# Where the weight buffers and the token buffers start within a partition

## The chip, the core and the metric

The kernel runs on one core of a Trainium2 chip. The metric is the device time of one execution in microseconds (us), the median of three runs; smaller is better. The engines are TensorE (PE for its matmuls, PEld for its weight loads), VectorE (DVE), ScalarE (ACT), GpSimd (POOL) and SyncE (SP), which issues most transfers.

## The reference, cut to what matters

The program is a two-layer decoder trunk on 512 tokens of width 1024. Each layer is a half-step feed-forward block, a mixing block (attention heads with an output projection) and a second feed-forward block, each followed by a normalisation:

```python
def swiglu(x, w_gu, w_down):
    g, u = jnp.split(x @ w_gu, 2, axis=-1)
    return (jax.nn.silu(g) * u) @ w_down

for layer in range(DEPTH):                       # DEPTH = 2
    x = layer_norm(DN_ALPHA * x + 0.5 * swiglu(x, ffn_w_gu[layer, 0], ffn_w_down[layer, 0]), ...)
    ...                                          # layer 0: latent attention; layer 1: sparse attention
    x = layer_norm(DN_ALPHA * x + mix, ...)
    x = layer_norm(DN_ALPHA * x + 0.5 * swiglu(x, ffn_w_gu[layer, 1], ffn_w_down[layer, 1]), ...)
```

All data is float32. The hidden width of the feed-forward block is 2816, or 22 blocks of 128.

## The kernel before, in words

**Precision.** Every large product is made of float32 numbers split into a high and a low part (`split`, L198 and L199: ACT rounds the high part, DVE subtracts it), and three of the four partial products are summed in PSUM. So one product is three matmuls: high by high, high by low, low by high.

**Weights.** `load` brings one unit of weights, 128 partitions by 1024 numbers, into one of the four buffers of `wraw`; `prep` splits it into a pair `whi`, `wlo` out of `wring` (three pairs) or, inside a scope, out of `wx` (four more pairs). `ahead` keeps this a few units in front of TensorE.

**Feed-forward.** For most blocks of 128 hidden features `seven` makes the gate and up products in quarters, by a scheme of seven products instead of eight, from sums of the weights and sums of the tokens (`token_forms`, the tiles named `t`): `quarter` (L366, L367, L370) runs matmuls whose stationary operand is a 128x128 piece of `whi` or `wlo` and whose moving operand is 256 tokens of `xhi`, `xlo` or a form `t`. The other blocks go through `feature_major` (L353, L355, L358), with the same roles. The down product goes through `prod` (L401 to L406): there the stationary operand is a piece of the hidden activations (`hhi`, `hlo`) and the moving operand is 512 columns of `whi` or `wlo`. The output projection of the mixing block uses `prod` too, with the tiles `mix` as stationary operand. Where it is the last tile of 128 tokens that is projected, the same products are written with `mm3` (L345 to L347).

**Where the buffers lie.** A partition holds 448 times 512 bytes. Pools stack up from the bottom (left side) or from the top (right side), each tile as long as its row, and the addresses below are those of the program as built. From the bottom lie a 4096-byte ring of descriptors (`DMA_RING`), four one-number constants of 32 bytes each, then `cst` (400 numbers, 1600 bytes) and `cbf` (384 bf16 numbers, 768 bytes). `wraw` therefore starts at 4096 + 128 + 1600 + 768 = 6592, which is 448 above a multiple of 512 (64 below the next). Every later tile on the left up to the extra pairs `wx` is a multiple of 512 bytes long, so all of `wraw`, `whi` and `wlo` start 448 above a multiple of 512, and so do the tiles of the attention heads that are opened on the left (`ke`, `ko`, `qt`, `va`, `sv`, `skc`, `pp`). In `open_f` a tile of 64 bytes named `offset` lies at the bottom of `xp`, in front of the tokens: `x`, `xhi`, `xlo`, the norm's gains and the forms `t` come out at 448 + 64 = 512, that is at a multiple of 512. On the right, `hhi`, `hlo`, `mix`, `cT` and the memory's `mhi`, `mlo` start at multiples of 512 and `qf` at 448. Below, the offset of a tile is its start modulo 512, and a pair such as 0/448 names the moving operand's offset first and the stationary operand's second. Inside a tile the matmuls begin at whole multiples of 512 bytes from its start, other than for the weights `wc` and `wgq`.

**Order.** The program places instructions in the order in which it is written; each engine runs its own in that order. The first transfer of `cst` is issued from POOL, and the bf16 copies `cbf` (L1252, L1253 in the trace) are made from it by DVE at the start.

Of the kernel before, what the change touches and what calls it, by code (L numbers as in the profile page):

```python
# [9 lines left out]
F32 = mybir.dt.float32  # L10
# [7 lines left out]
P = 128  # L18
# [85 lines left out]
def tile_trunk(ctx: ExitStack, tc, a: dict, out):  # L104
    nc = tc.nc
    order = _unit_order()

    const = ctx.enter_context(tc.tile_pool(name="const", bufs=1))
# [96 lines left out]
    def zero(t):  # L205
        nc.vector.memset(t.bitcast(F32), 0.0)

    cst = const.tile([P, 400], F32, name="cst")
    nc.gpsimd.dma_start(cst[:, 0:400], a["cst"])
    ident = cst[:, 0:128]  # L210
    valid = cst[:, 384:385]
    cbf = const.tile([P, 384], BF16, name="cbf")
    identb = cbf[:, 0:128]
    maskb = cbf[:, 128:256]
    maskb2 = cbf[:, 128:384]
    mhalf = cst[:, 385:387]

    class F:
        pass
# [1090 lines left out]
def _slopes(n):  # L1310
    def pow2(k):
        s = 2.0 ** (-8.0 / k)
        return [s ** (i + 1) for i in range(k)]
    c = 2 ** math.floor(math.log2(n))
    return np.asarray(pow2(c) + pow2(2 * c)[0::2][:n - c], np.float32)


def _round12(v):

    m, e = np.frexp(np.asarray(v, np.float64))  # L1320
    return np.ldexp(np.round(m * 4096.0) / 4096.0, e)


def _constants():

    f = np.float32
    c = {}
    cst = np.zeros((P, 400), f)
    cst[:, 0:128] = np.eye(P)
    i = np.arange(P)  # L1330
    cst[:, 128:256] = np.where(i[None, :] <= i[:, None], 0.0, NEG)
    cst[:, 384] = (i >= 31)
    cst[:, 385:387] = -0.5
    c["cst"] = cst

    freq = (f(10000.0) ** (-np.arange(16, dtype=f) / f(16))).astype(f)
    ang = (np.arange(T, dtype=f)[:, None] * freq[None, :]).astype(f)
    co, si = np.cos(ang.astype(np.float64)), np.sin(ang.astype(np.float64))
    rope = np.zeros((P, 2, NT, 32), f)
    ct = np.concatenate([co, co], 1).reshape(NT, P, 32).transpose(1, 0, 2)  # L1340
    sn = np.concatenate([-si, si], 1).reshape(NT, P, 32).transpose(1, 0, 2)
    rope[:, 0], rope[:, 1] = ct, sn
    c["rope"] = rope
    sc = 96.0 ** -0.5
    cs = np.zeros((P, 2, T), f)
    cosr = np.concatenate([co, co], 1).T * sc
    sinr = np.concatenate([-si, si], 1).T * sc
    cs[0:64, 0] = sc
    cs[64:96, 0], cs[96:128, 0] = cosr, sinr
    cs[0:32, 1], cs[32:64, 1] = cosr, sinr  # L1350
    cs[64:128, 1] = sc
    c["cs"] = cs

    pos = np.zeros(NKEY)
    for j in range(NT):
        for r in range(2):
            o = 256 * j + 128 * r
            pos[o:o + 128] = 128 * j + np.arange(128)
    alk = np.zeros((P, NKEY), f)
    for base in (0, 64):  # L1360
        for r in range(4):
            alk[base + r] = pos - (128 * r + 64)
        alk[base + 4:base + 6] = 1.0
        alk[base + 6:base + 12] = alk[base:base + 6]
    c["alk"] = alk
    m = _slopes(HEADS).astype(np.float64)
    tq = np.arange(T)
    alq = np.zeros((HEADS, 64, T), f)
    for h in range(HEADS):
        mh = _round12(m[h])  # L1370
        for r in range(4):
            alq[h, r] = np.where(tq // 128 == r, mh, 0.0)
            alq[h, 6 + r] = np.where(tq // 128 == r, m[h] - mh, 0.0)
        v = -m[h] * (tq - (128 * (tq // 128) + 64.0))
        v1 = _round12(v)
        v2 = _round12(v - v1)
        alq[h, 4], alq[h, 10] = v1, v2
        alq[h, 5] = _round12(v - v1 - v2)
    n = np.arange(32, dtype=f)
    dist = tq.astype(f)[:, None] - (n[None, :] * f(16.0) + f(15.5))  # L1380
    ok = (16 * n[None, :] + 31 <= tq[:, None]) & (n[None, :] < 31)
    alc = np.where(ok[:, None, :], -_slopes(HEADS)[None, :, None] * dist[:, None, :], f(NEG)).astype(f)
    c["alc"] = alc.reshape(NT, P, 2, 3, 2, 32).transpose(3, 1, 0, 4, 2, 5).reshape(3, P, T)
    c["alq"] = alq
    return c


def _layout(inp):
# [47 lines left out]
    o["cpos"] = g["cmp_pos"].reshape(2, 16, P).transpose(2, 0, 1)  # L1436
    o["cmp_b1"] = g["cmp_b1"].reshape(1, 2, 256)
    o.update(_constants())
    return {k: np.ascontiguousarray(v) for k, v in o.items()}

# [15 lines left out]
```

## Time and profile before

| what | value |
|---|---|
| median of 3 runs | 1913.37 us (1911.97 to 1915.62) |
| the profiled execution's own time | 1914.72 us |
| its span, from the first instruction to the last | 1912.8 us |
| TensorE's mean granted clock, as a share of full speed | 0.996 |
| PE busy, share of the span | 98% |
| PEld busy, share of the span | 87% |
| DVE / ACT / POOL busy, share of the span | 77% / 45% / 9% |
| matmuls | 12560 |

The busy time of a matmul in the profile overlaps with that of its neighbours, because matmuls are pipelined: what counts for the time is the distance from the start of one matmul to the start of the next. That distance is called the spacing below. It is read from the start times of a listing in order of time, or from the number of matmuls in a window of the trace. Such a number includes the one or two that were under way when the window began.

### The profile page before, as it was taken

Reading aid. Unit: us, or ns where it says so; the run is one execution under the profiler, and the core shown is the slowest. Engines: PE = TensorE matmul, PEld = TensorE weight load, DVE = VectorE, ACT = ScalarE, POOL = GpSimd, SP = SyncE. Lnnn points to the kernel's source line nnn. Section 1 sums busy time; section 2 is a strip of 40 time slices with the busy share of each in tenths; the row PEclk is TensorE's granted clock in tenths of the full one; section 3 lists DMA queues with packets and bytes.
Section 4 is the critical chain, followed back from the end, with each engine's and each line's share of the span. In section 5 each row is a group of like instructions: output and inputs, shape, how many; then the busy total and the mean of one; then the engine's idle time right before and its main releaser. Section 6 shows DMA issues by size and latency. Waiting matters only on the chain.

```text
span 1912.8 us, 31481 instructions
## 1 busy us (share of the span) xinstructions
PE 1883.7 (98%) x12560; PEld 1666.8 (87%) x12560; DVE 1470.0 (77%) x2363; ACT 870.1 (45%) x1435; POOL 164.3 (9%) x185
## 2 busy tenths in 40 slices
PE   9999999999999999999999999999999999999998
PEld 8899899886679899899989998998856689999997
DVE  7798788757658779778787987977477377887886
ACT  5344344446545335334653433444466344434432
POOL 0000000025500000000100000001255200000000
PEclk9999999999999999999999999999999999999999
DMA  6333334530134234234333323334421224323322
GB/s 235 111 111 101 120 100 143 174 106 32 59 110 134 77 100 133 78 100 144 123 110 110 121 87 100 122 105 161 111 45 27 101 77 132 105 84 111 113 79 74
DMA packets 59715, 203.88 MB, mean 107 GB/s; under 512 B 6945, under 2 KB 7217, under 8 KB 59569
## 3 DMA queue, kind: packets, MB, share of 16 engines
q1 hardware_dynamic: 57136, 194.70, 31.3%
q0 software_dynamic: 2432, 7.17, 1.2%
q8 instruction: 99, 1.62, 0.3%
q14 instruction: 48, 0.39, 0.1%
HBM read 188.21 MB, written 7.34 MB: 102 GB/s over the span
## 4 chain that ended last, share of the span: by engine, by line
PE 92%; DVE 3%; ACT 2%; issue 2%; POOL 1%; DMA 1%; POOLq 0%; DVEq 0%; ACTq 0%
PE bank L366 13%; PE bank L370 13%; PE bank L367 13%; PE bank L402 5%; PE bank L403 5%; PE bank L405 5%; PE bank L404 5%; PE bank L401 5%; PE bank L406 5%; PE bank L358 3%; PE bank L355 3%; PE bank L353 3%; PE o L634 3%; PE tb L606 3%; PE s L1136 1%
## 5 line engine op out<-in xcount | busy, mean ns | idle before, releaser
L198 ACT CAST whi<-wraw 128x1024 fp32r<-128x1024 f32 (+3 forms) x479 | 463.2, 974 | 585.9 <-PE bank L406 263.1
L199 DVE TENSOR_TENSOR wlo<-wraw,whi 128x1024 fp32r<-128x1024 f32 (+3 forms) x479 | 536.9, 1125 | 135.0 <-ACT whi L198 127.0
L366 PE MATMUL bank<-t,whi 128*128 128x256 f32 x1232 | 303.8, 279 | 0.0
L367 PE MATMUL bank<-t,whi 128*128 128x256 f32 x1232 | 303.6, 279 | 0.0
L366 PEld LDWEIGHTS bank<-t,whi 128*128 128x128 f32 x1232 | 231.1, 188 | 0.0
L367 PEld LDWEIGHTS bank<-t,whi 128*128 128x128 f32 x1232 | 231.0, 188 | 0.0
L366 PE MATMUL bank<-xhi,whi 128*128 128x256 f32 x924 | 227.9, 280 | 0.0
L367 PE MATMUL bank<-xlo,whi 128*128 128x256 f32 x924 | 227.7, 279 | 0.0
L370 PE MATMUL bank<-t,wlo 128*128 128x256 f32 x1232 | 194.8, 279 | 0.0
L366 PEld LDWEIGHTS bank<-xhi,whi 128*128 128x128 f32 x924 | 173.3, 188 | 0.8
L367 PEld LDWEIGHTS bank<-xlo,whi 128*128 128x128 f32 x924 | 173.3, 188 | 0.8
L370 PEld LDWEIGHTS bank<-t,wlo 128*128 128x128 f32 x1232 | 166.7, 188 | 0.0
L309 DVE SCALAR_TENSOR_TENSOR x<-x,bank 128x512 f32<-128x512 f32 x176 | 112.6, 682 | 70.3 <-PE bank L405 66.2
L370 PE MATMUL bank<-xhi,wlo 128*128 128x256 f32 x924 | 146.1, 279 | 0.0
L404 PE MATMUL bank<-wlo,hhi 128*128 128x512 f32 x336 | 132.9, 395 | 0.0
L402 PE MATMUL bank<-whi,hhi 128*128 128x512 f32 x336 | 132.7, 395 | 0.0
L406 PE MATMUL bank<-whi,hlo 128*128 128x512 f32 x336 | 132.7, 395 | 0.0
L405 PE MATMUL bank<-whi,hlo 128*128 128x512 f32 x336 | 132.5, 394 | 0.0
L403 PE MATMUL bank<-wlo,hhi 128*128 128x512 f32 x336 | 132.4, 394 | 0.0
L401 PE MATMUL bank<-whi,hhi 128*128 128x512 f32 x336 | 132.3, 394 | 0.0
L353 PE MATMUL bank<-xhi,whi 128*128 128x256 f32 (+1 forms) x472 | 127.8, 302 | 2.0 <-ACT xhi L198 2.0
L355 PE MATMUL bank<-xlo,whi 128*128 128x256 f32 (+1 forms) x472 | 127.6, 302 | 0.6 <-DVE xlo L199 0.6
(331 smaller groups left out, 3520.2 us busy)
## 6 DMA issues: line engine op xcount, KB each, us to landing
wraw<-in_gu SPq DMA_DIRECT2D x175, 512.0 KB, 3.4
wraw<-in_dn SPq DMA_DIRECT2D x88, 512.0 KB, 3.9
wraw<-in_wo SPq DMA_DIRECT2D x16, 512.0 KB, 3.6
wraw<-in_wm SPq DMA_DIRECT2D x8, 512.0 KB, 4.1
x_dram<-x SPq DMA_DIRECT2D x8, 512.0 KB, 2.8
x<-x_dram SPq DMA_DIRECT2D x8, 512.0 KB, 4.3
wraw<-in_w SPq DMA_DIRECT2D x8, 512.0 KB, 4.5
wraw<-in_wq SPq DMA_DIRECT2D x6, 512.0 KB, 4.2
```

Of the source, the lines that this page charges most:

```text
L198: nc.scalar.copy(hi, src)
L199: eng.tensor_tensor(lo, src, hi.bitcast(F32), op=ALU.subtract)
L353: nc.tensor.matmul(ps[:, c0:c1], lhsT=hi[:, k * P:(k + 1) * P], rhs=F.xhi[:, k, c0:c1], start=k == 0, stop=False)
L366: nc.tensor.matmul(ps, lhsT=hi[:, ks], rhs=xh[:, k], start=k == 0, stop=False)
L367: nc.tensor.matmul(ps, lhsT=hi[:, ks], rhs=xl[:, k], start=False, stop=False)
L370: nc.tensor.matmul(ps, lhsT=lo[:, ks], rhs=xh[:, k], start=False, stop=k == 3)
L401: nc.tensor.matmul(p0, lhsT=ahi, rhs=hi[:, 0:512], start=first, stop=False)
L402: nc.tensor.matmul(p1, lhsT=ahi, rhs=hi[:, 512:1024], start=first, stop=False)
L403: nc.tensor.matmul(p0, lhsT=ahi, rhs=lo[:, 0:512], start=False, stop=False)
L404: nc.tensor.matmul(p1, lhsT=ahi, rhs=lo[:, 512:1024], start=False, stop=False)
L405: nc.tensor.matmul(p0, lhsT=alo, rhs=hi[:, 0:512], start=False, stop=last)
L406: nc.tensor.matmul(p1, lhsT=alo, rhs=hi[:, 512:1024], start=False, stop=last)
```

## The change

The constants' tile `cst` loses the 128 columns (256 to 383) that nothing reads, and 16 columns that held three numbers are kept behind the rest, so that it has 288 columns, or 1152 bytes, instead of 400, or 1600 bytes. The transfer that fills it is as much smaller: 147,456 bytes instead of 204,800. No instruction is added or removed, and none changes its order.

By that every tile on the left behind `cst` starts 448 bytes lower: `wraw` at 6144, a multiple of 512, and so `whi`, `wlo`, and the heads' tiles on the left; the tokens `x`, `xhi`, `xlo` and the forms `t` come out 64 above a multiple of 512. Nothing moves on the right.

```diff
-    cst = const.tile([P, 400], F32, name="cst")
-    nc.gpsimd.dma_start(cst[:, 0:400], a["cst"])
+    cst = const.tile([P, 288], F32, name="cst")
+    nc.gpsimd.dma_start(cst, a["cst"])
     ident = cst[:, 0:128]
-    valid = cst[:, 384:385]
+    valid = cst[:, 256:257]
...
-    mhalf = cst[:, 385:387]
+    mhalf = cst[:, 257:259]
...
-    cst = np.zeros((P, 400), f)
+    cst = np.zeros((P, 288), f)
...
-    cst[:, 384] = (i >= 31)
-    cst[:, 385:387] = -0.5
+    cst[:, 256] = (i >= 31)
+    cst[:, 257:259] = -0.5
```

The pairs of offsets, moving/stationary, before and after:

| matmuls | before | after |
|---|---|---|
| gate and up: L366, L367, L370, L353, L355, L358 | 0/448 | 64/0 |
| down and output projection: L401 to L406, and `mm3` with `hhi`, `mix` | 448/0 | 0/0 |
| memory keys; memory values | 0/448; 448/0 | 0/0; 0/0 |
| `wc` (the two halves of a unit) | 448/0 and 64/0 | 0/64 and 128/64 |
| block scores with `skc`, `qf` | 448/448 | 448/0 |

## Rows read from the trace of the kernel before

**Rows 1.** The page: span and busiest engine (busy us, share, instructions).

```profile
span 1912.8 us, 31481 instructions
...
PE 1883.7 (98%) x12560; PEld 1666.8 (87%) x12560; DVE 1470.0 (77%) x2363; ACT 870.1 (45%) x1435; POOL 164.3 (9%) x185
```

**Rows 2.** The page: the chain of work that ended last, shares by engine.

```profile
PE 92%; DVE 3%; ACT 2%; issue 2%; POOL 1%; DMA 1%; POOLq 0%; DVEq 0%; ACTq 0%
```

**Rows 3.** Groups by line and shape: out<-in, xcount | busy us, mean ns | idle.

```profile
L366 PE MATMUL bank<-t,whi 128*128 128x256 f32 x1232 | 303.8, 279 | 0.0
...
L366 PE MATMUL bank<-xhi,whi 128*128 128x256 f32 x924 | 227.9, 280 | 0.0
...
L401 PE MATMUL bank<-whi,hhi 128*128 128x512 f32 x336 | 132.3, 394 | 0.0
...
L353 PE MATMUL bank<-xhi,whi 128*128 128x256 f32 x400 | 98.0, 283 | 2.0 <-ACT xhi L198 2.0
...
L401 PE MATMUL bank<-whi,mix 128*128 128x512 f32 x54 | 22.7, 421 | 0.0
```

**Rows 4.** Windows, PE alone: stretch, its length, busy (xmatmuls), clock, DMA share.

```profile
core 0: us, PE busy (x), PEclk, DMA share, GB/s
...
155.00:203.00 48.00, 48.00 (x410) 1.00 0.47 154
204.00:231.00 27.00, 27.00 (x118) 1.00 0.16 53
572.70:581.50 8.80, 8.80 (x80) 1.00 0.07 18
```

**Rows 5.** In order of time, PE: start us, us; down product, ten spacings.

```profile
133.66 0.39 PE L402 MATMUL bank<-whi,hhi 128*128 128x512 f32 x1
...
135.99 0.39 PE L406 MATMUL bank<-whi,hlo 128*128 128x512 f32 x1
```

**Rows 6.** In order of time, PE: gate-like product on 512 tokens, eleven spacings.

```profile
1361.37 0.39 PE L353 MATMUL bank<-xhi,whi 128*128 128x512 f32 x1
...
1363.88 0.39 PE L355 MATMUL bank<-xlo,whi 128*128 128x512 f32 x1
```

**Rows 7.** In order of time, PE: block scores with both operands at 448, five spacings.

```profile
1370.51 0.40 PE L346 MATMUL bank<-qf,skc 128*128 128x512 f32 x1
...
1371.67 0.39 PE L353 MATMUL bank<-xhi,whi 128*128 128x512 f32 x1
```

**Rows 8.** In order of time: memory scores, both operands at 0, five spacings.

```profile
417.44 0.28 PE L346 MATMUL s<-mix 128*128 128x256 f32 x1
...
418.04 0.34 PE L345 MATMUL j<-whi,cT 128*128 128x384 f32 x1
```

**Rows 9.** In order of time, PE: `wc`, second half of a unit, then first half.

```profile
383.40 0.35 PE L345 MATMUL bank<-whi,xhi 128*128 128x416 f32 x1
...
383.97 0.35 PE L345 MATMUL bank<-whi,xhi 128*128 128x416 f32 x1
...
384.53 0.35 PE L345 MATMUL bank<-whi,xhi 128*128 128x416 f32 x1
```

**Rows 10.** In order of time, PE: memory values, 448/0, six spacings.

```profile
365.00 0.28 PE L345 MATMUL bank<-whi,mhi 128*128 128x256 f32 x1
...
365.68 0.28 PE L345 MATMUL bank<-whi,mhi 128*128 128x256 f32 x1
```

**Rows 11.** One line's instructions, L345: duration ns min/median/max, first and last start, forms.

```profile
L345 PE MATMUL bank<-whi,hhi x32: 393/394/481, 351.1 to 1904.1; 128*128 128x512 f32 x32
...
L345 PE MATMUL bank<-whi,mix x20: 393/396/476, 564.6 to 1556.6; 128*128 128x512 f32 x20
```

**Rows 12.** In order of time, the first 10 us: [idle before <-releaser].

```profile
6.93 0.29 DVE L1252 CAST cbf<-cst 128x256 bf16<-128x256 f32 x1 [5.80 <-DMA cst<-in_cst]
...
7.58 2.56 ACT L198 CAST xhi<-b 128x512 fp32r<-128x512 f32 x4 [2.62 <-DMA b<-in_xT]
...
8.48 1.89 DVE L199 TENSOR_TENSOR xlo<-b,xhi 128x512 fp32r<-128x512 f32 x3
```

## The prediction

> **What bounds the kernel now.** I read the page's busy times first, then the chain of waits, the groups by shape, and then starts of matmuls in order of time. TensorE is busy for 1883.7 of 1912.8 us, the next engine for 77% [rows 1], and 92% of the chain that ended last is TensorE's own work [rows 2]. So the time is the number of matmuls times the distance between their starts. The reader should not use the 279 or 394 ns of a matmul in the groups [rows 3]: neighbours overlap. The spacing is what counts. In a long stretch of gate and up products 410 matmuls, less the two that were under way, fill 48.00 us: 117.6 ns each. In a stretch of down products it is 27.00 / 116 = 232.8 ns [rows 4], and by ten starts 2.33 / 10 = 233.0 ns [rows 5]. No other instruction is waited for in these stretches: PE is busy for the whole of each window [rows 4].
>
> The change adds, removes and reorders no instruction. It can act in two ways: by the spacing, if that depends on where operands start, and by the smaller first transfer.
>
> **Does the spacing depend on offsets at all?** Matmuls of one shape, at the same granted clock, run at different spacings. With 256 columns: 117.6 ns in the long stretch and 8.80 / 78 = 112.8 ns in another [rows 4], both 0/448; 0.68 / 6 = 113.3 ns at 448/0 [rows 10]; 0.60 / 5 = 120.0 ns at 0/0 [rows 8]. With 512 columns: 233.0 ns at 448/0 [rows 5]; 2.51 / 11 = 228.2 ns at 0/448 [rows 6]; 1.16 / 5 = 232.0 ns at 448/448 [rows 7]. So a few per cent are in play, and they don't follow the shape. But 112.8 and 117.6 ns stand at the same pair, so the offset alone doesn't fix the spacing; a stretch seems to settle into one rhythm and keep it. Traffic may have a part: the slow 256-column stretch had a DMA share of 0.47 and the fast one 0.07 [rows 4].
>
> I take as working idea that what matters is where the stream of moving columns stands against the weight load that runs beside it, so the difference of the two offsets. It is no more than an idea; the rows bear it out in part.
>
> **Part 1, gate and up products.** Their count is 3 x (1232 + 924) + 3 x 400 = 7668 matmuls of 256 columns (L366, L367 and L370 have equal counts, as have L353, L355 and L358) [rows 3]. The pair goes from 0/448 to 64/0. The difference is 64 before and after (modulo 512). By the working idea nothing changes: 0. The bounds: if all settle into the fast rhythm, 7668 x (117.6 - 112.8) = -36.8 us. For the other side the nearest row is `wc`, where matmuls of one chain, with the same stationary tile, run at 0.57 / 3 = 190 ns with 64/0 and at 0.56 / 3 = 187 ns with 448/0 [rows 9]. That is the pair that these products get, and it is the slower by 1.6%: 7668 x 117.6 x 0.016 = +14.4 us. I take 0, as the long stretch itself is the nearest row and its difference is kept.
>
> **Part 2, down and output projections.** There are 6 x (336 + 54) = 2340 matmuls in `prod` [rows 3] and 3 x (32 + 20) = 156 in `mm3` [rows 11], 2496 in all, with 512 columns. They go from 448/0 to 0/0, so the difference goes from 448 to 0. The nearest row with 512 columns and difference 0 is the block scores at 448/448: 232.0 ns [rows 7]. Sum: 2496 x (232.0 - 233.0) = -2.5 us. Bounds: the best 512-column spacing in the trace, 228.2 ns with a moving operand at 0 [rows 6], gives 2496 x 4.8 = -12.0 us. On the other side, the 256-column row with difference 0 is the slowest of its shape, 120.0 ns, 2.4 ns over the usual one [rows 8]; as an addition to 233.0 it would be +6.0 us. I take the row with the same shape.
>
> **Part 3, the small products.** The memory values are 2 layers x 2 tiles x 8 pieces x 3 = 96 matmuls that go from 448/0 to 0/0: 96 x (120.0 - 113.3) = +0.6 us [rows 8, 10]. The memory keys, 96 more from 117.6 to 120.0, give +0.2 us [rows 4, 8]. `wc`, `wgq`, the scores of the first layer and half of those of the second keep their difference; the heads wait for other engines in part. 0 for those.
>
> **Part 4, the first transfer.** DVE stands in front of its first copy until `cst` has landed, at 6.93 us, and the split of the first tokens stands behind it and the weights' splits at 8.48 us. The tokens' high part, made by ACT from 7.58 us in four pieces of 2.56 / 4 = 0.64 us, is there at 8.22 [rows 12]. So a `cst` that lands earlier brings at most 8.48 - 8.22 = 0.26 us, and at the least nothing. I take -0.1 us. The order of the queues stays: nothing is moved past anything on SP or POOL.
>
> **Part 5, engines beside TensorE.** ACT and DVE read and write the same tiles at new offsets. DVE's share is 77% in the mean [rows 1], and PE is busy throughout the windows [rows 4], so a change there is hidden behind matmuls, unless DVE became slower by a quarter (0.77 x 1.3 = 1). 0.
>
> **Sum.** -2.5 + 0.6 + 0.2 - 0.1 = -1.8 us. Against the profiled execution's own 1914.72 us (1912.8 us of span and 1.9 around it) that is 1912.9; the median of the runs lies 1.35 us lower, so the forecast is 1913.37 - 1.8 = 1911.6 us. About 0.2% (3.8 us) is what a measurement of this kernel can tell from no change, so this is a forecast of no change that could be told.
>
> **The rivals.**
> Rival A, slower. The moving operand's own offset decides, and 64 is worse than 0 or 448, as in `wc` [rows 9]. Then the gate and up products pay 14.4 us: 1911.6 + 14.4 = 1926.0 us. The point from which it decides: a loss of 1.8 / 7668 = 0.23 ns for each of them eats the gain. For it: the pair 64/0 is exactly theirs. Against it: in `wc` the two pairs alternate every three matmuls, so no rhythm can settle, and the spacing there may belong to the switch. Chance 0.22.
> Rival B, faster by the down products. A moving operand at 0 runs at the 228.2 ns of rows 6: -12.0 + 0.7 gives 1902.1 us. For it: both kinds with 512 columns and an operand at 448 that moves are slower [rows 5, 7] than the one at 0 [rows 6]. Against it: the stationary operand differs too. Chance 0.19.
> Rival C, the gate and up stretches fall into the fast rhythm: 1911.6 - 36.8 = 1874.8 us if all did. The trace has that rhythm at this very difference [rows 4], but only in a short stretch. Chance 0.04.
> Rival D, the change doesn't do anything: offsets don't enter, and the different spacings come from elsewhere, the traffic for one. 1913.3 us. Chance 0.10.
> The Trainium skill, "TensorE: Matmul & The Clock Gate", section "Step-by-step: what each phase is for", says that the array has two separate read ports, so that loading the next weights takes nothing from the matmul in flight. By that rule the difference of the offsets could not count, and rival D's time would follow. This case's trace doesn't decide it, though 228.2 against 233.0 ns at one shape and clock is hard to fit to it.
>
> **How the numbers follow.** The forecast has a chance of 0.45, with a range of its own from 1907 (the down products at 231 ns) to 1914 (no gain there). Of it 0.14 lies over 0.2% faster, 0.28 within, 0.03 slower. With B and C faster: 0.37. With D the same: 0.38. With A slower: 0.25. The range that leaves out C, and half of the two ends, is 1899 to 1927.
>
> **What would show each step.** In the profile after: the number of matmuls in the windows of gate and up stretches (410 in 48 us if part 1 holds, about 404 by rival A, 427 by C); ten starts of down products (2.32 us by the forecast, 2.28 by B, 2.33 by D); memory values at 120 instead of 113 ns; the first copy of `cst` a little before 6.93 us. The prediction is wrong if the spacing of the 7668 gate and up matmuls moves by more than half a nanosecond either way, since that is 3.8 us, all that the measurement can tell.

## The result and the profile after

| | before | after |
|---|---|---|
| median | 1914.36 us (1911.97 to 1915.62, 4 runs) | 1900.43 us (1899.25 to 1901.54, 4 runs) |
| ratio, with its 95% interval | | 0.9929 [0.9911, 0.9946] |
| the profiled execution's own time, and its span | 1914.72 us, 1912.8 us | 1899.25 us, 1897.3 us |
| TensorE's mean granted clock | 0.996 | 0.996 |

The change makes the kernel 0.7% faster. The forecast of 1911.6 us, no change that could be told, was 11.2 us too high; the time lies inside its range, near the lower end.

The page of the kernel after, with the lines that answer to [rows 1, 2]:

```profile
span 1897.3 us, 31481 instructions
...
PE 1867.9 (98%) x12560; PEld 1666.4 (88%) x12560; DVE 1468.1 (77%) x2363; ACT 870.2 (46%) x1435; POOL 164.3 (9%) x185
...
PE 92%; DVE 3%; ACT 2%; POOL 1%; issue 1%; DMA 0%; POOLq 0%; DVEq 0%; ACTq 0%
```

The count of instructions is that of before, and each share is within a point of that before. PE's busy time fell by 15.8 us and the span by 15.5, so what was gained was gained on TensorE. The groups by line and shape say where (line engine op, out<-in, xcount | busy us, mean ns | idle):

```profile
L366 PE MATMUL bank<-t,whi 128*128 128x256 f32 x1232 | 303.5, 279 | 0.0
...
L401 PE MATMUL bank<-whi,hhi 128*128 128x512 f32 x336 | 131.0, 390 | 0.0
```

Against [rows 3] the gate product has its 279 ns still, the down product 390 instead of 394. Those durations overlap, so the spacing has to say it. The windows of the kernel after, PE alone (columns as in [rows 4]):

```profile
core 0: us, PE busy (x), PEclk, DMA share, GB/s
153.00:201.00 48.00, 48.00 (x410) 1.00 0.47 154
...
202.00:228.00 26.00, 26.00 (x116) 1.00 0.16 54
...
568.70:577.50 8.80, 8.80 (x77) 1.00 0.05 19
...
992.00:1019.00 27.00, 27.00 (x241) 1.00 0.51 161
```

The stretch of gate and up products holds 410 matmuls in 48 us, exactly as in [rows 4]. Of the other stretches of 40 gate and up products or more, three changed their rhythm. One, of 252 products from 991.41 us, runs at 27.00 / 239 = 113.0 ns here and at 117.8 in the kernel before. Two short ones went the other way: the 81 products of which [rows 4] have 80 in 8.80 us have 77 in that time here, and 58 products (from 1337.23 us before, from 1325.19 after) went from 114.9 to 119.2 ns. The listing in order of time (start us, us, engine, line, operation, tiles; in brackets the idle time before and its releaser) has the head, ten spacings of down products, the opening of a stretch of down products and eighty spacings further on in it, and the memory values:

```profile
6.29 0.29 DVE L1252 CAST cbf<-cst 128x256 bf16<-128x256 f32 x1 [5.16 <-DMA cst<-in_cst]
...
6.79 2.59 ACT L198 CAST xhi<-b 128x512 fp32r<-128x512 f32 x4 [1.58 <-DMA b<-in_xT]
...
133.22 0.39 PE L401 MATMUL bank<-whi,hhi 128*128 128x512 f32 x1
...
135.49 0.39 PE L405 MATMUL bank<-whi,hlo 128*128 128x512 f32 x1
...
201.73 0.40 PE L401 MATMUL bank<-whi,hhi 128*128 128x512 f32 x1
...
203.12 0.39 PE L401 MATMUL bank<-whi,hhi 128*128 128x512 f32 x1
...
207.66 0.39 PE L403 MATMUL bank<-wlo,hhi 128*128 128x512 f32 x1
...
225.79 0.39 PE L405 MATMUL bank<-whi,hlo 128*128 128x512 f32 x1
...
363.77 0.28 PE L345 MATMUL bank<-whi,mhi 128*128 128x256 f32 x1
...
364.49 0.28 PE L345 MATMUL bank<-whi,mhi 128*128 128x256 f32 x1
```

Ten spacings of down products take 2.27 us, where [rows 5] have 2.33. Eighty take 18.13 us: 226.6 ns each. But the stretch opens more slowly: its first six spacings, from 201.73 us, take 1.39 us, or 232 ns each. The memory values take 0.72 / 6 = 120 ns, where [rows 10] have 113.3.

Both kernels run the same matmuls in the same order. So the distance from each start to the next can be subtracted pair by pair, and the 15.5 us of the two spans come apart by what the matmul works on (after minus before, us; a distance counts for the matmul at its start; the same for three of the kernels below):

| matmuls | distances | after | E5 | E1 | E2 |
|---|---|---|---|---|---|
| down products, with `hhi` or `hlo` | 2111 | -12.59 | -0.01 | -12.64 | -12.71 |
| output projection, with `mix` | 384 | -1.57 | 0.00 | -1.64 | -1.53 |
| gate and up, with `xhi`, `xlo`, `t` | 7884 | -0.26 | +1.16 | -1.20 | +17.06 |
| memory keys and values | 192 | +0.46 | -0.03 | +0.48 | +0.47 |
| up to the first gate product | 12 | -0.79 | -1.05 | -1.24 | -0.85 |
| all else, waits among it | 1976 | -0.76 | +1.01 | +0.17 | +1.11 |
| sum | 12559 | -15.51 | +1.08 | -16.07 | +3.55 |

Of the gain, 14.2 us lie in the 2495 down and output projections, 5.7 ns for each (14.8 us if a distance counts for the matmul at its end). That is less than the 233.3 - 226.6 = 6.7 ns of the long stretches (E5 and E1 below), in part because every stretch of down products opens with the slower spacings.

### The profile page after: what moved, and what is told of

It reads as the page before. It is cut to its first block, busy times and chain, and to the rows that moved or that the text cites. A ratio compares the mean times of both kernels' runs of the same rounds, so it can differ in the third digit from the quotient of the medians.

```text
span 1897.3 us, 31481 instructions
## 1 busy us (share of the span) xinstructions
PE 1867.9 (98%) x12560; PEld 1666.4 (88%) x12560; DVE 1468.1 (77%) x2363; ACT 870.2 (46%) x1435; POOL 164.3 (9%) x185
## 4 chain that ended last, share of the span: by engine, by line
PE 92%; DVE 3%; ACT 2%; POOL 1%; issue 1%; DMA 0%; POOLq 0%; DVEq 0%; ACTq 0%
PE bank L366 13%; PE bank L370 13%; PE bank L367 13%; PE bank L405 4%; PE bank L401 4%; PE bank L402 4%; PE bank L403 4%; PE bank L404 4%; PE bank L406 4%; PE bank L358 3%; PE bank L355 3%; PE bank L353 3%; PE o L634 3%; PE tb L606 3%; PE s L1136 1%; PE bank L347 1%
## 5 line engine op out<-in xcount | busy, mean ns | idle before, releaser
L366 PE MATMUL bank<-t,whi 128*128 128x256 f32 x1232 | 303.5, 279 | 0.0
L367 PE MATMUL bank<-t,whi 128*128 128x256 f32 x1232 | 303.2, 279 | 0.0
L366 PEld LDWEIGHTS bank<-t,whi 128*128 128x128 f32 x1232 | 231.1, 188 | 0.0
L367 PEld LDWEIGHTS bank<-t,whi 128*128 128x128 f32 x1232 | 231.0, 187 | 0.0
L366 PE MATMUL bank<-xhi,whi 128*128 128x256 f32 x924 | 227.7, 280 | 0.0
L367 PE MATMUL bank<-xlo,whi 128*128 128x256 f32 x924 | 227.5, 279 | 0.0
L370 PE MATMUL bank<-t,wlo 128*128 128x256 f32 x1232 | 194.6, 279 | 0.0
L366 PEld LDWEIGHTS bank<-xhi,whi 128*128 128x128 f32 x924 | 173.4, 188 | 0.7
L367 PEld LDWEIGHTS bank<-xlo,whi 128*128 128x128 f32 x924 | 173.2, 187 | 0.7
L370 PEld LDWEIGHTS bank<-t,wlo 128*128 128x128 f32 x1232 | 166.6, 188 | 0.0
L309 DVE SCALAR_TENSOR_TENSOR x<-x,bank 128x512 f32<-128x512 f32 x176 | 112.5, 681 | 62.5 <-PE bank L405 58.8
L370 PE MATMUL bank<-xhi,wlo 128*128 128x256 f32 x924 | 145.9, 279 | 0.0
L401 PE MATMUL bank<-whi,hhi 128*128 128x512 f32 x336 | 131.0, 390 | 0.0
L406 PE MATMUL bank<-whi,hlo 128*128 128x512 f32 x336 | 130.8, 389 | 0.0
L353 PE MATMUL bank<-xhi,whi 128*128 128x256 f32 (+1 forms) x472 | 128.3, 303 | 1.7 <-ACT xhi L198 1.7
L355 PE MATMUL bank<-xlo,whi 128*128 128x256 f32 (+1 forms) x472 | 128.0, 302 | 0.7 <-DVE xlo L199 0.7
```

Source lines behind the costliest of these rows:

```text
L353: nc.tensor.matmul(ps[:, c0:c1], lhsT=hi[:, k * P:(k + 1) * P], rhs=F.xhi[:, k, c0:c1], start=k == 0, stop=False)
L366: nc.tensor.matmul(ps, lhsT=hi[:, ks], rhs=xh[:, k], start=k == 0, stop=False)
L367: nc.tensor.matmul(ps, lhsT=hi[:, ks], rhs=xl[:, k], start=False, stop=False)
L370: nc.tensor.matmul(ps, lhsT=lo[:, ks], rhs=xh[:, k], start=False, stop=k == 3)
L401: nc.tensor.matmul(p0, lhsT=ahi, rhs=hi[:, 0:512], start=first, stop=False)
L406: nc.tensor.matmul(p1, lhsT=alo, rhs=hi[:, 512:1024], start=False, stop=last)
```

## The experiments

Each kernel is the one after with one or two sizes changed. The time stands beside one run of the kernel before on the same chip, other than in E12, which has several runs of both. "Difference" is the moving operand's start less the stationary operand's.

**E5. The smaller transfer alone.** `cst` is cut, but to 272 columns instead of 288, which leaves every later tile at its offset of before.

```diff
-    cst = const.tile([P, 288], F32, name="cst")
+    cst = const.tile([P, 272], F32, name="cst")
...
-    cst = np.zeros((P, 288), f)
+    cst = np.zeros((P, 272), f)
```

> The constants cut to 272 columns, 512 bytes less than before, so that every start modulo 512 is as in the kernel before: only the smaller first transfer is left of the change. Both theories: all spacings as before, and at most 0.26 us less in the first 10 us: 1914 us. Theory 3 (the gain comes from something other than the starts modulo 512, such as the first transfer): 1900 us.

Measured: 1915.81 us, before 1915.6. One row of its listing and its windows:

```profile
6.05 0.29 DVE L1252 CAST cbf<-cst 128x256 bf16<-128x256 f32 x1 [4.92 <-DMA cst<-in_cst]
```

```profile
core 0: us, PE busy (x), PEclk, DMA share, GB/s
7.00:15.00 8.00, 7.05 (x34) 0.57 1.04 407
...
1403.00:1413.00 10.00, 7.90 (x35) 0.83 0.19 44
...
155.00:203.00 48.00, 48.00 (x410) 1.00 0.45 154
205.00:231.00 26.00, 26.00 (x114) 1.00 0.13 44
```

The same two windows of the kernel before:

```profile
core 0: us, PE busy (x), PEclk, DMA share, GB/s
7.00:15.00 8.00, 6.16 (x37) 0.79 1.04 413
...
1403.00:1413.00 10.00, 7.90 (x45) 1.00 0.18 44
```

The head starts earlier (the first copy at 6.05 us, 6.93 in [rows 12]), but in this execution nothing of it is left. From 7 to 15 us the granted clock is 0.57 of full speed, where the same window of before has 0.79, so more of the first products run at 1.2 GHz instead of 2.4; the window has 37 matmuls before, 34 here. At 58 us this kernel stands 0.26 us behind before, and at the start of each stretch of gate and up products until 933 us it is 0.25 to 0.28. Around two pauses of the attention the clock differs again: 1.7 us are gained near 975 us and 2.2 lost near 1410 us, where the window from 1403 us has 0.83 and before 1.00.

The loss at the head doesn't come with the smaller transfer as such. E1 below has the same one, and its granted clock in that window is 1.00:

```profile
7.00:15.00 8.00, 6.90 (x48) 1.00 1.02 399
```

Its first product starts 1.24 us earlier than before, and at the end of the first stretch it is 1.39 us ahead (62.94 us against 64.33). So what the earlier start is worth went by the clock, 0.26 us lost here and some 1.2 us kept in E1; the time of one run tells neither. With the offsets of before the down and projection products keep their spacing to 0.01 us in all 2495: in 26 us this kernel has 114 of them, the kernel after 116.

**E1. Difference or the moving operand's own offset.** `cst` as in E5, and the tile `rest` 64 bytes longer, so that `hhi`, `hlo` and `mix` start at 448: down 448/448, gate and up 0/448.

```diff
-    cst = const.tile([P, 288], F32, name="cst")
+    cst = const.tile([P, 272], F32, name="cst")
...
-    small.tile([P, 24], F32, name="rest")
+    small.tile([P, 40], F32, name="rest")
```

> The small constants, but weights at 448 and tokens at 0 as in the kernel before, and all of the right side moved 64 bytes down, so that hhi, hlo and mix start at 448 as well: the down products are 448/448, the gate and up products 0/448. Theory 1 (the difference of the two offsets sets the spacing): the down products run at the 227 ns that they have after the change at 0/0, and the time is 1914 - 15 = 1899 us. Theory 2 (the moving operand's own offset sets it, 0 being good): they stay at 233 ns and the time stays at 1914 us. Gate and up products stay at 117.7 ns by both.

Measured: 1898.65 us, before 1915.6. Eighty spacings of down products in its listing:

```profile
207.74 0.39 PE L406 MATMUL bank<-whi,hlo 128*128 128x512 f32 x1
...
225.87 0.39 PE L402 MATMUL bank<-whi,hhi 128*128 128x512 f32 x1
```

Again 18.13 / 80 = 226.6 ns, with both operands 448 above the grid. At 448/0, in E5, 78 spacings from 207.65 to 225.85 us are 18.20 / 78 = 233.3 ns. The moving operand is at 448 in both, the stationary one at 0 in the slow kernel before and in the fast kernel after. Neither start decides by itself; the two together do, and both fast pairs have the difference 0. The gain of the change is had with the weights off the 512-byte grid too.

**E2. The gate and up products at difference 0.** The tile `offset` is left out: gate and up 0/0, down 0/0.

```diff
-        F.xp.tile([P, 16], F32, name="offset")
```

> The kernel after, without the 64-byte tile in front of the tokens: gate and up products are 0/0. Theory 1 (the difference): as in the memory scores of before, 120.0 instead of 117.7 ns, so 1900 + 7668 x 0.0023 = 1918 us. Theory 2 (the moving operand's own offset): 0 is the best, so 117.7 ns or less, 1900 us or down to 1866. Down products stay at 227 ns by both.

Measured: 1918.2 us, before 1915.6. A window of gate and up products:

```profile
155.00:204.00 49.00, 49.00 (x410) 1.00 0.45 152
```

That is 49.00 / 408 = 120.1 ns. The column E2 of the table above shows the two effects side by side: the down products keep their gain, and the gate and up products lose 17.1 us. The moving operand's own start doesn't decide with 256 columns either: it is at 0 here and in E5, where the stationary one at 448 gives 410 matmuls in 48 us. Difference 0 is the better one for 512 columns and the worse one for 256.

**E4. The gate and up products at difference 448**, the difference at which the memory values ran at 113.3 ns [rows 10].

```diff
-        F.xp.tile([P, 16], F32, name="offset")
+        F.xp.tile([P, 112], F32, name="offset")
```

> The kernel after with the tile in front of the tokens grown from 64 to 448 bytes: gate and up products are 448/0. Theory 1 (the difference): the memory values of before had this difference, 448, and ran at 113.3 ns, so 1900 - 7668 x 0.0044 = 1866 us. Theory 2 (the moving operand's own offset): a moving operand at 448 was the slow one in the down products of before (3% over), so 117.7 ns or up to 121, 1900 to 1925 us. Down products stay at 227 ns by both.

Measured: 1896.45 us, before 1915.6. Its windows:

```profile
core 0: us, PE busy (x), PEclk, DMA share, GB/s
44.00:62.00 18.00, 18.00 (x161) 1.00 0.58 195
...
151.50:200.00 48.50, 48.50 (x414) 1.00 0.45 154
```

The time of 1866 us that theory 1 gave didn't come. Two rhythms stand at one pair of offsets: 18.00 / 159 = 113.2 ns in the first stretch of a feed-forward block, and 48.50 / 412 = 117.7 ns after its first down product. The DMA share is higher in the fast one (0.58 against 0.45), so traffic doesn't make the slow one.

**E6, E7, E3, E8. The differences 128, 192, 256, 320.** Only the length of `offset` changes: 32, 48, 64 and 80 numbers.

```diff
-        F.xp.tile([P, 16], F32, name="offset")
+        F.xp.tile([P, 48], F32, name="offset")     # E7
```

> The kernel after with the tokens at 128 instead of 64: gate and up products 128/0, down products 0/0 as before. Theory 1 (the difference of the two offsets; 0 is the worst for 256 columns at 120 ns, 64 and 448 give 113.3 or 117.7 ns by how a stretch begins): further away it is 113.3 ns throughout, 1900 - 7668 x 0.0044 = 1866 us. Theory 1b (a stretch takes its rhythm from what runs ahead of it, and behind a down product it is always the slow one): 117.7 ns, 1896 to 1900 us. Wherever it comes out, the down products stay at 227 ns.

> The same with the tokens at 192: gate and up products 192/0. Theory 1: 113.3 ns, 1866 us. Theory 1b: 117.7 ns, 1896 to 1900 us.

> The same with the tokens at 256, half of 512 away from the weights: gate and up products 256/0. The only row with this difference so far, a product with a stationary operand of 64 columns in the kernel after, ran at 113.3 ns. Theory 1: 113.3 ns, 1866 us. Theory 1b: 117.7 ns, 1896 to 1900 us.

> The same with the tokens at 320: gate and up products 320/0. Theory 1: 113.3 ns, 1866 us. Theory 1b: 117.7 ns, 1896 to 1900 us.

Measured: E6 1918.01, E7 1895.79, E3 1919.57, E8 1900.25 us, before 1916.5. What they expected of a larger distance fell: 256 behaves as 0 (1918.2 us), 320 as 64 (1900.43), and 192 as 448 (1896.45). The pattern repeats every 256 bytes. The windows of E3 and of E8:

```profile
156.00:205.00 49.00, 49.00 (x411) 1.00 0.45 152
```

```profile
152.50:201.50 49.00, 49.00 (x419) 1.00 0.45 155
```

In 49 us E3 starts 411 matmuls and E8 419, eight more: 119.8 and 117.5 ns.

**E10, E9, E11. The differences 160, 224 and 96**, to see whether the steps between follow their neighbours (theory 3), or whether half a step of 64 bytes keeps the two streams apart (theory 4): `offset` of 40, 56 and 24 numbers.

> The kernel after with the tokens at 160: gate and up products 160/0, a difference that is an odd multiple of 32. Theory 3 (the difference modulo 256 decides, smoothly: 120 ns at 0 and 128, 117.7 at 64, 113.3 or 117.7 at 192): between 128 and 192, so 117 to 119 ns and 1896 to 1912 us. Theory 4 (the streams meet where the difference is a whole number of 64-byte steps, and half a step keeps them apart): 113.3 ns throughout, 1866 us.

> The same with the tokens at 224. Theory 3: between 192 and 256 (which is 0), so 117 to 119 ns, 1896 to 1912 us. Theory 4: 113.3 ns throughout, 1866 us.

> The same with the tokens at 96. Theory 3: between 64 and 128, so 118 to 119 ns, 1902 to 1912 us. Theory 4: 113.3 ns throughout, 1866 us.

Measured: E10 1911.08, E9 1908.01, E11 1920.38 us, before 1915.66. Theory 4's 1866 us came in none. E10 and E9 lie between their neighbours, as theory 3 says; E11 doesn't, it runs at the 120.0 ns of difference 128. The windows of E9 and E11:

```profile
154.00:203.00 49.00, 49.00 (x416) 1.00 0.47 154
```

```profile
154.50:204.00 49.50, 49.50 (x415) 1.00 0.47 152
```

They give 49.00 / 414 = 118.4 and 49.50 / 413 = 119.9 ns. All differences together, by starts in the listings: some 260 spacings of gate and up products in the stretch at 160 to 191 us, and 16 spacings of the 512-column products of `feature_major` near 990 us (first and last start in us; the values for 512 columns are exact to about 0.6 ns).

| difference | kernel | 256 columns | ns | 512 columns | ns |
|---|---|---|---|---|---|
| 0 | E2 | 159.73 to 191.05, 261 | 120.0 | 994.65 to 998.28 | 226.9 |
| 64 | after | 159.80 to 190.66, 262 | 117.8 | 985.92 to 989.58 | 228.8 |
| 96 | E11 | 159.79 to 190.75, 258 | 120.0 | 996.00 to 999.73 | 233.1 |
| 128 | E6 | 159.82 to 191.26, 262 | 120.0 | 994.44 to 998.15 | 231.9 |
| 160 | E10 | 159.80 to 190.77, 261 | 118.7 | 990.64 to 994.39 | 234.4 |
| 192 | E7 | 159.73 to 190.59, 262 | 117.8 | 982.15 to 985.88 | 233.1 |
| 224 | E9 | 159.80 to 190.68, 261 | 118.3 | 989.88 to 993.61 | 233.1 |
| 256 | E3 | 159.76 to 190.84, 259 | 120.0 | 995.96 to 999.59 | 226.9 |
| 320 | E8 | 159.80 to 190.66, 262 | 117.8 | 985.82 to 989.48 | 228.8 |
| 448 | E4 | 159.75 to 190.61, 262 | 117.8 | 984.06 to 987.79 | 233.1 |
| 192, first stretch | E7 | 43.77 to 61.90, 160 | 113.3 | | |
| 448, first stretch | E4 | 43.79 to 61.92, 160 | 113.3 | | |

The stretch at 160 us follows down products. Others can run differently at the same difference: in E6 the 375 products from 583.04 us, ahead of the block's first down product, take 118.9 ns each.

**E12. The best of them, timed.** The kernel of E7 (weights and down products as after, tokens 192 above the grid), in several runs.

> The kernel with the tokens at 192 once more, timed in rounds beside the kernel before. Theory 3: about 1896 us, a ratio of 0.990 to the kernel before, some 4 us less than the kernel after, all of it from stretches that begin after a pause of TensorE and run at 113.3 ns. If the single look was an accident of how the stretches began: the kernel after's ratio of 0.993.

Measured: 1896.51 us (1895.54 to 1899.65, 4 runs) against 1914.28 (7 runs), a ratio of 0.9912 [0.9895, 0.9929]. Its windows:

```profile
core 0: us, PE busy (x), PEclk, DMA share, GB/s
44.00:62.00 18.00, 18.00 (x162) 1.00 0.58 196
...
151.50:200.00 48.50, 48.50 (x415) 1.00 0.47 153
...
579.00:600.00 21.00, 21.00 (x188) 1.00 0.41 126
```

The first stretches of the blocks run at 18.00 / 160 = 112.5 and 21.00 / 186 = 112.9 ns, the later one at 48.50 / 413 = 117.4. Short stretches are less steady. One window of E7, and the same of E12:

```profile
923.50:934.00 10.50, 10.50 (x95) 1.00 0.29 102
```

```profile
923.50:934.00 10.50, 10.50 (x91) 1.00 0.33 108
```

That is 112.9 and 118.0 ns in two executions of one kernel. By distances its gate and up products take 4.3 us less than in the kernel after, and its whole span 3.7 us less. It, E7 (the same kernel) and E4 lie within 0.8 us of each other, and every other version was slower. The intervals of the two ratios overlap, so its lead of 0.2% over the kernel after is borne by the traces and not told apart by the times.

## Why the prediction came out as it did

**What bounds the kernel.** Right. The time follows the spacing on TensorE, stretch by stretch, and no other engine came in. In the traces the gain is 15.5 us where 1.8 were forecast. Of the 13.7 us between them, by the table of distances, 11.7 lie in part 2; parts 1, 3 and 4 have 0.3, 0.3 and 0.7, and waits and all else, which the forecast had at nothing, 0.8.

**The working idea, the difference of the two offsets.** Right in E1 and in the kernel after, with one correction: it counts modulo 256 bytes, not 512 (E3, E8). For the pairs of this change both give the same.

**Part 1, gate and up.** The term of 0 held: 410 matmuls in 48 us, and -0.26 us over 7884 distances (the forecast's 7668, and 216 of 512 columns). That small sum hides the three stretches that changed their rhythm: the one from 991.41 us fell into the fast one, as rival C had it for all, and gained 1.1 us; the two short ones lost it, for 0.6 us together. At difference 64 the offsets don't settle which rhythm such a stretch takes: E5, with the offsets of before, has the 81 products in the slow one too (77 in 8.80 us).

**Part 2, down and output projection.** This is the step that failed, by its size. It took 2496 x 1.0 ns = -2.5 us and measured -14.2 us. The 232.0 ns of [rows 7] came from five spacings in a run of six products, the last of the five already into the next product; the four before it, from 1370.51 to 1371.45 us, take 235 ns each. A run of six is too short to price a stretch: the down stretch of the kernel after opens with six spacings of 232 ns too, at difference 0, and only behind them runs at 226.6. Whether the scores would have come down in the same way isn't shown. Even the bound of 228.2 ns from [rows 6] was too high, as that row has difference 64: in the table above 64 gives 228.8 and 0 gives 226.9. The row was chosen for its shape and its pair, which was sound, and not for its length. The end of 1907 us, given for 231 ns, doesn't follow from the forecast's own sum: 2496 x 2.0 ns is 5.0 us, which with the 0.7 us of the other parts makes 1909.1. That the range holds the measured time is luck in part, since its lower end was drawn below rival B, whose reason fell.

**Part 3, memory products.** The sign held and the spacing of 120 ns came as said. +0.8 us was forecast for the two kinds; +0.46 was measured, or +0.74 with a distance counted for the matmul at its end.

**Part 4, the first transfer.** The bound of 0.26 us was too small for the head: the first copy came 0.64 us earlier and the tokens' split 0.79 us, since the transfer of `xT` landed earlier too, which the bound had held fixed. In the trace of the kernel after these 0.79 us are kept: the first stretch of gate and up products takes 56.07 us in both kernels. E1 kept its 1.24 us as well. E5 shows that such an earlier start needn't reach the end: there 1.05 us went into products at a lower clock. So the term was too small by some 0.7 us in this trace, which is less than what the runs of one kernel scatter by.

**The rivals.** A falls: gate and up at 64/0 run as at 0/448, and the 190 ns of `wc` [rows 9] say nothing on a long stretch. D falls: the interval of the ratio leaves out 1, and the spacing moves with the offsets. B's 1902.1 us is near the time, but its reason is not the one: it had the moving operand's own start at 0 decide, and E1 has the same 226.6 ns with that start at 448. C had the right rhythm and the wrong place for it: E4 and E12, at other differences, show it throughout the first stretches of the blocks only, and the kernel after in one of them.

The Trainium skill's rule of two separate read ports ("TensorE: Matmul & The Clock Gate", section "Step-by-step: what each phase is for"), by which, as rival D had it, the difference couldn't count, doesn't fit the runs: with one shape, one order and a granted clock of 1.00, down products stand 233.3 ns apart in E5 and 226.6 in E1. What makes it so, the runs don't show.

## What to carry to other kernels

Where TensorE is busy throughout, the start of the moving operand against that of the stationary one was worth 3% of a product's time with 512 columns and 2% with 256 here, and it can be moved by a tile of a few bytes; the best difference must be sought for each shape, since 0 was best for 512 columns and among the worst for 256. To price such a change, read the spacing over a hundred matmuls of a stretch that has run in, not over five. And subtract the starts of two traces with equal order, matmul by matmul: it separates an effect of 6 ns from clock and waits, which moved single runs by 1 to 2 us.

## What the runs showed of the hardware

- The spacing depends on the difference of the operands' starts (0/0 and 448/448 both 226.6 ns, 448/0 233.3), and repeats every 256 bytes: E2 and E3 both 120.0 and 226.9 ns, after and E8 both 117.8 and 228.8 ns.
- The two shapes want opposite things: difference 0 gives the shortest spacing with 512 columns and the longest with 256. Why is open.
- One difference can have two stable rhythms with 256 columns: 113.3 and 117.8 ns at 64, 192 and 448. Behind down products all 16 long stretches (336 or 420 products) ran slow in each of these kernels. The four other long ones, each ahead of a block's first down product, ran fast at 192 and 448 (E4, E7, E12); one of them, from 987.75 us in E7, follows gate products of 512 columns without a pause. Short stretches took either, differently even in two executions of one kernel (E7 and E12, from 923.5 us). What decides is open, and what a short break between down and gate products would do wasn't tried.
- At difference 0 a stretch of down products needs some six spacings to settle: 232 ns each from 201.73 us in the kernel after, then 226.6.
- An earlier start of 1.05 us at the head was lost in E5, where the clock stayed at its lower level for longer (0.57 against 0.79 in the mean from 7 to 15 us); one of 1.24 us was kept in E1, at 1.00.
